# Weight sums written over the weight tiles, other step sequences and adding transfers in an encoder layer's blocked products

## The chip, the cores and the metric

The kernel runs on one core of one Trainium2 chip. The metric is the device time of one execution in microseconds (us). The engines that matter are TensorE (PE, matrix products into PSUM banks), VectorE (DVE) and ScalarE (ACT, both elementwise), GpSimd (POOL) and SyncE (SP), whose queue issues most transfers. Each engine takes its instructions in order; semaphores tie the engines together.

## The reference

One encoder layer over 256 tokens of 4096 features, all in float32. A combined projection feeds two groups of attention heads, latent attention and dilated attention; their gated outputs are mapped back and added, and a gated per-layer embedding and a last norm follow.

```python
h = rms_norm(x, g_mix[i])
proj = jnp.einsum('bsd,de->bse', h, w_in[i])
c_q, c_kv, k_rope, gate_a, q_b, k_b, v_b, gate_b = jnp.split(proj, split_idx, axis=-1)
...
y_a = rms_norm(y_a.reshape(B, S, MLA_WIDTH), g_out_mla[i]) * jax.nn.silu(gate_a)
...
y_b = rms_norm(y_b.reshape(B, S, DIL_WIDTH).astype(x.dtype), g_out_dil[i]) * jax.nn.silu(gate_b)
x = x + jnp.einsum('bse,ed->bsd', jnp.concatenate([y_a, y_b], axis=-1), w_out[i])
ple = jnp.einsum('bsc,cd->bsd', p[i], w_ple[i])
gate = jax.nn.sigmoid(jnp.einsum('bsd,de->bse', rms_norm(x, g_ple[i]), w_ple_gate[i]))
x = x + ple * gate
return rms_norm(x, g_final)
```

The widths are 4096 to 11840 columns for `w_in`, 4096 to 4096 for `w_out` and `w_ple_gate`.

## The kernel before

**Products.** Each float32 operand is split into a high part `hi` (rounded on ACT) and a low part `lo` (the rest, on DVE), and a product is three matmuls: hi by hi, hi by lo, lo by hi (`mm`, line 263). The activations are the stationary side, 128 by 128; the weights stream, 512 columns at a time.

**Blocks and steps.** A `Block` (line 1152) is 256 tokens by 1024 columns, with 32 weight rows of 128 (kt). Its four quarters are two token halves t by two column halves h. A plain step (`plain_step`, line 1194) loads one weight row (128 by 1024), converts it (one ACT instruction of 1024 columns, one on DVE) and does four products into the banks M2, X, M3 and M4. A fast pair (`fast_steps`, line 1215) takes two weight rows as a 2 by 2 matrix of 512 columns each and needs seven products instead of eight, by the Winograd form of Strassen's scheme, into M1 to M7. For that it needs four sums of weight pieces, made on DVE from the two loaded tiles into a tile T (`split1`, `split2`), and four sums of pieces of the left side, made once for a family of blocks (`add_sums`, line 1256). A pair is four steps: M1; M2 and M3; M5 and M7; M6 and M4. The first needs both loads, and both load buffers are free after the second; the last two convert from T. After the last fast step `d_mid` (line 1012), `gate_mid`, `out_mid` or `wide_mid` combine the banks M1, M5, M6 and M7 into the four quarters; after the last step `d_done` (line 1042), `gate_done`, `out_done` or `wide_done` add the other four banks.

**Order.** There are 18 such blocks: six for q, k and v of the dilated group (two of each), five gate and latent blocks, three output blocks and four of the embedding gate, with attention and smaller products between them. `spread` (line 1644) lays out the steps of a block: some plain ones as lead, then pair steps f and plain steps c mixed evenly by their cost on DVE, then plain ones as trail; e stands for the two steps of the embedding's product. The pairs per block stand in `FAST_QKV`, `FAST_G`, `FAST_O` and `FAST_P`: 3, 7, 8, 8, 8, 7; 3, 6, 7, 7, 7; 6, 7, 6; 7, 7, 7, 5. Instructions are issued by a planner that runs at build time: a clock (`Clock`, line 68) models each engine, steps are converted some steps ahead of PE (`convert_one`, line 1965), and other work is fitted in between as tasks that yield (`advance`, line 427).

**Buffers.** Weight rows are loaded by SP into four buffers `raw` of 2 by 512 columns (`fetch`, line 1951). The tile T of a pair is `T5` and `T6` in the q, k, v blocks, `B1` in the gate blocks, `B4` and `Al1` in the output blocks and `Ah2` in the last four. The high and low parts go to a ring of three tile pairs and to whatever larger tiles are free at that stage.

**Profile names.** All matmuls and most other instructions carry line 177, the helper that records them. `m`, `s`, `o` and `t` are PSUM banks, `raw` the load buffers, `hi` and `lo` the ring; `B`, `Ah`, `Al` and `T` are tiles of SBUF with their numbers left out.

Of the kernel before, what the change touches and what calls it, by code (L numbers as in the profile page):

```python
# [12 lines left out]
F32 = mybir.dt.float32  # L13
# [6 lines left out]
P = 128  # L20
S = 256
# [13 lines left out]
WARM = 6, 3  # L35

# [31 lines left out]
class Clock:  # L68


    SEEN = {"pe": 0.21, "act": 0.13, "dve": 0.125, "pool": 0.1, "sp": 0.0}

# [48 lines left out]
    def run(self, engine, us, outs, ins, late=0.0):  # L121
# [6 lines left out]
        if late:  # L128
            queue = "dma", engine
            self.free[queue] = max(self.free.get(queue, 0.0), at + 2.0) + late  # L130
            seen = self.free[queue]
        else:
            seen = at + us + self.SEEN[engine]
# [7 lines left out]
class Metered:  # L141
# [5 lines left out]
    def __getattr__(self, op):  # L147
        do = getattr(self.engine, op)

        def emit(out, *rest, **named):  # L150
# [11 lines left out]
            if op == "dma_start":  # L162
                us, late = (0.06 if key == "sp" else 1.0), out.shape[0] * size(out) * 4 / 400e3
                ins = []
# [46 lines left out]
def encoder_layer(ctx: ExitStack, tc: tile.TileContext, x, p, positions, g_mix, w_in, g_q_latent, w_uq,  # L211
# [30 lines left out]
    def plain(t):  # L242
        return t.bitcast(F32)

# [344 lines left out]
    def attend(h, q_src, k_src, pe, v, y, dil):  # L589
# [96 lines left out]
        nc.scalar.activation(y, by_token(o) if dil else o, AF.Copy)  # L686
# [16 lines left out]
    def head_unit(name, load, product, tags, done, n=2, time=48 * 0.119):  # L703
# [3 lines left out]
        def step(j):  # L707
            box = []

            def get():  # L710
                box.append(clock.made(wp.tile([P, 2, Q], F32, tag="raw", name=f"raw_{name}_{j}", bufs=RAW), "raw", RAW))
                load(box[0], j)
# [11 lines left out]
            new.ring, new.ring_id = HEADS_RING, "heads"  # L724
# [104 lines left out]
    def turn_steps(n, tags):  # L829
# [4 lines left out]
        def step(j):  # L834
            box = []

            def load():
                box.append(clock.made(wp.tile([P, 2, Q], F32, tag="raw", name=f"raw_r{n}_{j}", bufs=RAW), "raw", RAW))
# [19 lines left out]
            new.ring, new.ring_id = HEADS_RING, "heads"  # L858
# [53 lines left out]
    def gate_rest(dil, c, u):  # L912
# [6 lines left out]
        for b in range(2):  # L919
# [9 lines left out]
            for k in range(2):  # L929
                h = 4 * c + 2 * b + k  # L930
                g = G["ob" if dil else "oa"][:, h:h + 1]
                y = yb_rows(h) if dil else by_token(y_rows(ya, h))
                nc.vector.scalar_tensor_tensor(y, y, g, by_token(tp[:, k]), op0=ALU.mult, op1=ALU.mult)
# [3 lines left out]
    QUARTERS = (0, 0, "M2"), (1, 1, "X"), (0, 1, "M3"), (1, 0, "M4")  # L937

    def gate_mid(tags, blk, after=()):

        def task():
# [9 lines left out]
            for d, a, b in (((1, 1), (0, 0), "M6"), ((1, 0), (1, 1), "M5"), ((0, 1), (1, 1), "M7"),  # L951
                            ((1, 1), (0, 1), "M5")):
                nc.vector.tensor_tensor(e[d[0]][:, d[1]], e[a[0]][:, a[1]], ps[b], op=ALU.add)
# [58 lines left out]
    def d_mid(key, blk):  # L1012
        def task():
# [11 lines left out]
            yield from awaited("rx")  # L1025
            sc = [(rxq if key[0] == "q" else rx)[:, t:t + 1] for t in range(NT)]

            def add(h, t, m, old):
# [1049 lines left out]
```

## Time and profile before

| what | value |
|---|---|
| time of the runs, median (lowest to highest) | 1900.07 us (1898.4 to 1900.59), 3 runs |
| profiled execution: first to last instruction, its span | 1897.4 us |
| mean granted TensorE clock | 0.998 |
| busy: PE, DVE, ACT, POOL | 1878.5, 1696.8, 1140.2, 31.2 us |
| bytes moved by DMA | 370.59 MB |

The span runs from the first to the last instruction of the program; the profiled execution has no other time than this one. The time of a run has a little more around it, so the median stands 2.7 us above the span. Busy times are unions of an engine's instruction spans. Matmuls are pipelined and their ends are modelled, so their spans overlap and are longer than their distance.

### The profile page before, as it was taken

What the parts mean: (1) busy time and instruction counts of PE and PEld (TensorE: products, weight loads), DVE (VectorE), ACT (ScalarE), POOL (GpSimd) and SP (SyncE); (2) the same over time, 40 slices, a digit from 0 to 9 for tenths busy, and PEclk for the clock granted to TensorE, in tenths of its full rate; (3) what the DMA queues carried; (4) which work ended last, traced back from release to release, by engine and by line L of the source; (5) the groups of instructions that cost most, each with busy time, mean ns of one, the idle gap of its engine ahead of it and who ended that gap; (6) DMA issues with size and microseconds to landing.
All of it is one profiled execution on the core that took longest, in us unless ns stands there. A gap on an engine that the chain in (4) does not pass through costs nothing.

```text
span 1897.4 us, 25417 instructions
## 1 busy us (share of the span) xinstructions
PE 1878.5 (99%) x9133; PEld 1579.8 (83%) x9133; DVE 1696.8 (89%) x2354; ACT 1140.2 (60%) x1543; POOL 31.2 (2%) x41
## 2 busy tenths in 40 slices
PE   9999999999999999999999999999999999999997
PEld 7888888888899888888888999888888888888885
DVE  6999999899898989999998777999989989989897
ACT  7655656565588555556556556656655555666654
POOL 0000000000011000000000010100000000000000
PEclk9999999999999999999999999999999999999999
DMA  8666666666735566666667553576666666665665
GB/s 279 189 205 213 214 212 200 198 213 193 218 84 159 166 211 183 196 215 189 208 199 209 137 142 123 167 231 204 216 199 217 187 194 218 194 223 183 221 222 180
DMA packets 160871, 370.59 MB, mean 195 GB/s; under 512 B 29116, under 2 KB 70952, under 8 KB 160744
## 3 DMA queue, kind: packets, MB, share of 16 engines
q1 hardware_dynamic: 159896, 366.58, 62.0%
q0 software_dynamic: 512, 1.84, 0.3%
q8 instruction: 72, 1.18, 0.3%
q10 hardware_dynamic: 336, 0.54, 0.1%
q14 instruction: 55, 0.45, 0.1%
HBM read 364.72 MB, written 4.19 MB: 194 GB/s over the span
## 4 chain that ended last, share of the span: by engine, by line
PE 85%; DVE 10%; DMA 2%; issue 2%; ACT 1%; POOL 0%; DVEq 0%; ACTq 0%; POOLq 0%
PE m L177 49%; PE t L177 16%; PE s L177 11%; PE o L177 9%; DVE lo L177 3%; DVE B L177 3%; DVE T L177 2%; DVE Ah L177 1%; DMA raw<-in_w_ple_gate_dram 1%; DVE Al L177 1%; DMA raw<-in_w_in_dram 1%; ACT hi L177 0%; DVE st L177 0%; ACT B L177 0%; DVE B7b L177 0%
## 5 line engine op out<-in xcount | busy, mean ns | idle before, releaser
L177 ACT ACTIVATE hi<-raw 128x1024 fp32r<-128x1024 f32 (+2 forms) x396 | 378.9, 966 | 278.1 <-PE m L177 70.9
L177 DVE TENSOR_TENSOR lo<-raw,hi 128x1024 fp32r<-128x1024 f32 (+2 forms) x396 | 433.4, 1107 | 61.8 <-ACT hi L177 60.6
L177 PE MATMUL m<-hi,Ah 128*128 128x512 f32 (+2 forms) x659 | 247.2, 387 | 0.3 <-ACT hi L177 0.3
L177 DVE TENSOR_TENSOR B<-raw,B 128x1024 fp32r<-128x1024 f32 (+3 forms) x228 | 213.9, 947 | 20.5 <-ACT B L177 18.8
L177 PE MATMUL m<-hi,Al 128*128 128x512 f32 (+2 forms) x625 | 229.6, 380 | 0.0
L177 PE MATMUL m<-lo,Ah 128*128 128x512 f32 (+2 forms) x549 | 207.8, 379 | 1.4 <-DVE lo L177 1.3
L177 ACT ACTIVATE B<-raw 128x1024 fp32r<-128x1024 f32 (+2 forms) x142 | 135.3, 962 | 96.8 <-DMA raw<-in_w_in_dram 25.3
L177 PE MATMUL m<-hi,B 128*128 128x512 f32 (+1 forms) x524 | 179.0, 389 | 0.0
L177 PE MATMUL m<-B,Ah 128*128 128x512 f32 (+2 forms) x554 | 146.7, 359 | 0.6 <-DVE B7b L177 0.6
L177 PEld LDWEIGHTS m<-hi,Ah 128*128 128x128 f32 x659 | 124.0, 188 | 22.7 <-ACT hi L177 1.2
L177 PEld LDWEIGHTS m<-hi,Al 128*128 128x128 f32 x625 | 117.5, 188 | 21.8
L177 PEld LDWEIGHTS m<-lo,Ah 128*128 128x128 f32 x549 | 103.4, 188 | 19.9 <-DVE lo L177 2.9
L177 PEld LDWEIGHTS m<-hi,B 128*128 128x128 f32 x524 | 98.2, 188 | 19.6
L177 PEld LDWEIGHTS m<-B,Ah 128*128 128x128 f32 x554 | 95.9, 189 | 15.3 <-DVE B7b L177 1.0
L177 PE MATMUL m<-lo,B 128*128 128x512 f32 (+1 forms) x262 | 102.1, 390 | 0.1
L177 PE MATMUL m<-B,Al 128*128 128x512 f32 (+2 forms) x289 | 99.1, 371 | 0.0
L177 DVE TENSOR_TENSOR T<-raw,T 128x512 f32<-128x512 f32 (+2 forms) x110 | 85.5, 789 | 3.3 <-ACT T L177 1.7
L177 ACT ACTIVATE hi<-B 128x1024 fp32r<-128x1024 f32 x57 | 59.4, 1056 | 23.1 <-PE m L177 7.3
L177 DVE TENSOR_TENSOR lo<-B,hi 128x1024 fp32r<-128x1024 f32 x57 | 68.5, 1220 | 3.9 <-ACT hi L177 3.6
L177 PE MATMUL t<-hi,Ah 128*128 128x512 f32 x184 | 69.9, 391 | 0.0
L177 ACT ACTIVATE B<-T 128x1024 fp32r<-128x1024 f32 (+2 forms) x55 | 50.2, 916 | 22.8 <-DVE T L177 13.4
L177 PEld LDWEIGHTS m<-B,Al 128*128 128x128 f32 x289 | 54.4, 188 | 9.2
(530 smaller groups left out, 4336.9 us busy)
## 6 DMA issues: line engine op xcount, KB each, us to landing
raw<-in_w_in_dram SPq DMA_DIRECT2D x359, 512.0 KB, 4.3
raw<-in_w_out_dram SPq DMA_DIRECT2D x128, 512.0 KB, 4.6
raw<-in_w_ple_gate_dram SPq DMA_DIRECT2D x128, 512.0 KB, 4.7
raw_q<-in_w_uq_dram SPq DMA_DIRECT2D x32, 256.0 KB, 3.8
T<-in_x_dram SPq DMA_DIRECT2D x13, 512.0 KB, 6.6
raw<-in_w_in_dram SPq DMA_DIRECT2D x16, 320.0 KB, 3.1
raw_r<-in_w_uq_dram SPq DMA_DIRECT2D x16, 256.0 KB, 4.3
raw_k<-in_w_ukv_dram SPq DMA_DIRECT2D x16, 256.0 KB, 3.4
```

What stands on the lines that cost most here:

```text
L177: return do(out, *rest, **named)
```

## The change

- The four weight sums of a pair are written over the two loaded tiles: first the two sums of the first tile, once its left half has been converted, then the two of the second, once it has been converted. Signs change so that most of these are additions; `mix` and the quarter sums take the other signs.
- The tile T is no longer used for sums; its stage lends it as two more load buffers (`lend`, `give_back`), so that there are six where there were four. The load buffers are now one tile with named places, and a pair holds its two until its third and fourth step are converted. If both places adjoin, the first two sums are one instruction.
- In 23 of the pairs (letter A) the first two sums are made by a transfer that POOL issues and that adds a part of the weights onto the first tile.
- `spread` gives way to step sequences written out: c is a plain step; a or A, b, g, h are the four steps of a pair; e is the embedding's product, now last in its block. Steps of two pairs may be mixed. The pairs are 2, 8, 8, 8, 8, 8; 3, 6, 8, 7, 8; 6, 7, 6; 8, 8, 8, 5.
- In the q, k, v and latent blocks the norm's scale is taken out of the bank sums and applied to the finished quarters, on DVE or ACT. The output gain is applied where attention writes its result, so the gating is one multiplication for two heads.
- The sums of the left side take four DVE instructions instead of five; sums beyond the room of before go over parts of the left side that only plain steps use.
- The planner's clock has other landing times for transfers and a longer issue on SP.

```diff
+ORDER_D = (
+    "ccccccccccccccccccacAcbcccghbghccccc",
+    "cccaccbghAccbcaghbcghcacbcaghbghcabgahbgcahbghcc",
+    "ccccabacbgcgchacbhcghcabccAghbabgcghhabgabhghccc",
+    "ccccacbghabghccabcabgchgahbcgabghcachcbgabghhccc",
+    "ccabgccccabghhacabgbhghccccabghabcgchaabbggchhcc",
+    "ccccccabagbghhcabghacbghaAccabgcchbgcbghhabcghcc",
+)
+ORDER_G = (
+    "ccccccccccccccacbgcchacbgcacbhgchccccc",
+    "ccAcccbgcAccbhcghccaccbagabhghccbgabghchcccc",
+    "cccccabccacgcbagbghchahbgaahcbcgbhgchcabgabghhcc",
+    "cccccacbaccgbhgahacbgccAhbghbcghcabcgcahbgchcc",
+    "cccacbgaahccbgcbgcahbaghchbcgcaAbbghhcgacchbghcc",
+)
+ORDER_O = (
+    "ccaacccbbggchcahcccacbccghbcghabacgbhgcchccc",
+    "ccacbcacgchbcgcAhAbbccgghcabchcgabhcgabhghcccc",
+    "ccccabccghcabgacchbcAcghbcacbggcahhbgccchccc",
+)
+ORDER_P = (
+    "cccaccAbgcbchcgabghachbcagbgchhAAbcbcghaghbghccce",
+    "ccAbcgccabcaghhbgchacbghacbcacbcghcgaAhbgbcghhcce",
+    "cAcbccgcAcbAhbghcagcchbcgaAhbbgchghcaAbbccgghhcce",
+    "ccccacAbcghbcAcbghghabgacchbghcccc",
+)
...
+    LANDS = {"sp": 2.3, "act": 2.0, "pool": 5.7}
...
+    RAW, NEAR = 4, 0.3
+    raw_all = wp.tile([P, 2 * RAW, 512], F32, tag="raw", name="raw_all", bufs=1)
+    raw_at = {i: (raw_all, 2 * i) for i in range(RAW)}
...
+    def next_to(a, b):
+        return raw_at[a][0] is raw_at[b][0] and raw_at[b][1] == raw_at[a][1] + 2
+
+    def lend(stage, tags):
+
+        if lent["stage"] != stage:
+            give_back()
+            lent["stage"] = stage
+            for tag, n in tags:
+                t = slot(tag, [2 * n, 512])
+                for i in range(n):
+                    raw_at[lent["n"]] = t, 2 * i
+                    raw_free.append(lent["n"])
+                    lent["n"] += 1
...
+    def mix(e, ps):
+
+        nc.vector.tensor_tensor(e(1, 1), e(0, 0), ps["M6"], op=ALU.add)
+        nc.vector.tensor_tensor(e(1, 0), ps["M5"], e(1, 1), op=ALU.subtract)
+        nc.vector.tensor_tensor(e(0, 1), e(1, 1), ps["M7"], op=ALU.subtract)
+        nc.vector.tensor_tensor(e(1, 1), ps["M5"], e(0, 1), op=ALU.subtract)
...
+            nc.scalar.activation(d[0][:, 0], ps["M1"], AF.Copy)
+            mix(lambda h, t: d[h][:, t], ps)
...
-                nc.vector.scalar_tensor_tensor(d[h][:, t], blk.ps[m], sc[t], d[h][:, t], op0=ALU.mult, op1=ALU.add)
+                nc.vector.tensor_tensor(d[h][:, t], blk.ps[m], d[h][:, t], op=ALU.add)
+            yield from awaited("rx")
+            for m, t, h in quarters[2:] + quarters[:2] if key == ("v", 1) else quarters:
+                if clock.free["dve"] + 0.3 < clock.free["act"]:
+                    nc.vector.tensor_scalar(d[h][:, t], d[h][:, t], sc[t], None, op0=ALU.mult)
+                else:
+                    nc.scalar.activation(d[h][:, t], d[h][:, t], AF.Copy, scale=sc[t])
...
             def split1(hi, lo):
-                if isinstance(self.tmp, tuple):
-                    T.extend(slot(b, [2, self.q]) for b in self.tmp)
-                else:
-                    both = slot(self.tmp, [4, self.q])
-                    T.extend((both[:, :2], both[:, 2:]))
-                sub(T[0][:, 0], r[0][:, 1], r[0][:, 0])
-                sub(T[0][:, 1], r[0][:, 1], r[1][:, 1])
                 split(hi[:, 0], lo[:, 0], r[0][:, 0])
+                if dma:
+                    at = self.row(2 * j) * P
+                    nc.gpsimd.dma_start(r[0], self.w[at:at + 2 * P, self.q:2 * self.q].rearrange("(k p) n -> p k n", p=P),
+                                        accum_op=ALU.add)
 
             def split2(hi, lo):
+                if dma:
+                    split(hi, lo, r[1])
+                    return
                 nc.scalar.activation(hi, r[1], AF.Copy)
-                sub(T[1][:, 0], r[1][:, 1], T[0][:, 0])
-                sub(T[1][:, 1], r[1][:, 0], T[1][:, 0])
+                if next_to(slots[0][0], slots[1][0]):
+                    t, h = raw_at[slots[0][0]]
+                    plus(r[0], t[:, h + 1:h + 2].to_broadcast([P, 2, self.q]), t[:, h:h + 4:3])
+                else:
+                    plus(r[0][:, 0], r[0][:, 1], r[0][:, 0])
+                    plus(r[0][:, 1], r[0][:, 1], r[1][:, 1])
                 nc.vector.tensor_tensor(lo, r[1], plain(hi), op=ALU.subtract)
+                sums34()
+
+            def sums34():
+                plus(r[1][:, 1], r[1][:, 1], r[0][:, 0])
+                plus(r[1][:, 0], r[1][:, 0], r[1][:, 1])
+
+            def split3(hi, lo):
+                nc.scalar.activation(hi, r[0], AF.Copy)
+                if dma:
+                    sums34()
+                nc.vector.tensor_tensor(lo, r[0], plain(hi), op=ALU.subtract)
...
-                two(ALU.add, u[:, 0], a[:, 1], a[:, 3])
-                two(ALU.subtract, u[:, 1], u[:, 0], a[:, 0])
-                two(ALU.subtract, u[:, 2], a[:, 1], a[:, 0])
-                two(ALU.subtract, u[:, 3], a[:, 2], u[:, 1])
+                two(ALU.subtract, u[:, 0:3:2], a[:, 1:2].to_broadcast([P, 2, P]), a[:, 0:4:3])
+                two(ALU.subtract, u[:, 1], u[:, 2], a[:, 0])
+                two(ALU.add, u[:, 3], a[:, 2], u[:, 1])
...
-    FAST_QKV, LEAD_QKV = (3, 7, 8, 8, 8, 7), (18, 4, 4, 4, 4, 4)
-    FAST_G, LEAD_G = (3, 6, 7, 7, 7), (15, 10, 6, 6, 4)
-    FAST_O, LEAD_O = (6, 7, 6), (4, 5, 4)
```

269 lines of the change are left out of this document (152 added, 117 removed).

## The prediction

> **What bounds the kernel now.** I read the page first (span, busy shares), then the chain of waits in order of time, then the stages, then what PE waits for. The page:
>
> ```profile
> span 1897.4 us, 25417 instructions
> PE 1878.5 (99%) x9133; PEld 1579.8 (83%) x9133; DVE 1696.8 (89%) x2354; ACT 1140.2 (60%) x1543; POOL 31.2 (2%) x41
> PEclk9999999999999999999999999999999999999999
> ```
>
> TensorE (PE) is busy all the time, at the full clock, and VectorE (DVE) is not far behind. A busy PE could still be slow, so the chain of waits is asked for its pace (start, length, what, how many):
>
> ```profile
> 1.46 2.74 PE m L177 x6
> 195.71 6.80 PE m L177 x30
> 1617.86 16.32 PE m L177 x72
> ```
>
> The first work of PE starts at 1.46 us. Thirty matmuls of 512 columns in 6.80 us and 72 in 16.32 us, 1400 us apart: 0.2267 us each, back to back. That is PE's pace where nothing holds it. A product of this kernel is three such matmuls, 0.68 us. The stages (start:end, length, then busy us of each engine with its count):
>
> ```profile
> 100.00:500.00 400.00, 399.35 (x1761) 329.85 (x1760) 379.85 (x454) 230.94 (x250) 0.69 (x1) 1.00 0.66 207
> 500.00:650.00 150.00, 149.89 (x981) 138.29 (x980) 130.06 (x277) 108.40 (x217) 12.82 (x15) 1.00 0.49 144
> 1100.00:1300.00 200.00, 198.53 (x1106) 171.16 (x1105) 166.99 (x265) 118.51 (x191) 13.66 (x14) 1.00 0.54 169
> 1600.00:1840.00 240.00, 240.00 (x1060) 198.75 (x1059) 219.66 (x260) 145.89 (x175) 0.00 (x0) 1.00 0.65 209
> 1840.00:1897.40 57.40, 43.69 (x211) 35.77 (x210) 43.92 (x75) 27.50 (x39) 0.00 (x0) 0.93 0.56 195
> ```
>
> PE idles 0.65 us of 400 in the first stage, although DVE is busy for 379.85 of them (95%); 1.47 us of 200 in the stage where the second attention passes into the output blocks; nothing from 1600 to 1840; and 13.71 us in the last stage, the drain behind the last products, which the change leaves alone. The waits that the profile names for PE are small:
>
> ```profile
> PE m L177 <- DVE lo L177: 1.3, 3, 0.8
> PE m L177 <- DVE B7b L177: 0.9, 2, 0.6
> PE m L177 <- DVE Al L177: 0.3, 1, 0.3
> ```
>
> So the time is PE's work. The span can fall only by fewer matmuls, or by these 2.5 us of waits for DVE and little else. DVE is the second limit: a pair costs it more than it saves PE, so what DVE can carry decides how many pairs are possible.
>
> **The change, part by part.** *Pairs.* Two plain steps (two weight rows kt) are 8 products; a fast pair of steps is 7. I count one pair for each letter h in the sequences. The blocks for q, k, v go from 41 to 42, the next five from 30 to 32, the output blocks stay at 19, the last four go from 26 to 29: 116 becomes 122. Six products less, 18 matmuls at 0.2267 us: **-4.08 us** of PE. Nothing hides this, since PE is the path; the transposes and the last steps keep their matmuls.
>
> *What a pair costs DVE and ACT.* The groups by shape (count, busy us, mean ns of one):
>
> ```profile
> L177 DVE TENSOR_TENSOR lo<-raw,hi 128x1024 fp32r<-128x1024 f32 x309 | 374.0, 1220 | 59.4 <-ACT hi L177 58.3
> L177 DVE TENSOR_TENSOR lo<-raw,hi 128x512 fp32r<-128x512 f32 x77 | 52.5, 684 | 1.0 <-ACT hi L177 0.9
> L177 DVE TENSOR_TENSOR B<-raw,B 128x512 f32<-128x512 f32 x86 | 59.2, 688 | 1.5
> L177 ACT ACTIVATE hi<-raw 128x1024 fp32r<-128x1024 f32 x309 | 323.8, 1058 | 240.9 <-PE m L177 64.7 <-DMA raw<-in_w_in_dram 52.7 <-PE t L177 48.1
> L177 ACT ACTIVATE hi<-raw 128x512 fp32r<-128x512 f32 x77 | 48.0, 625 | 37.2 <-PE t L177 11.5 <-PE o L177 7.9 <-issue 7.0
> ```
>
> Before, a pair is four sums of 512 columns, one low part of 512 and three of 1024 on DVE: 4 x 0.688 + 0.684 + 3 x 1.220 = 7.10 us, against 2 x 1.220 = 2.44 us for two plain steps. So six more pairs cost DVE 6 x 4.66 = +28.0 us. On ACT they cost 6 x (0.625 + 3 x 1.058 - 2 x 1.058) = +10 us, which its 40% idle time hides.
>
> *Adding transfers.* Each letter A (4 + 4 + 3 + 12 = 23) lets a DMA make the first two sums: 23 x 2 x 0.688 = **-31.6 us** of DVE. In the other 99 pairs, where the two weight tiles adjoin, the two sums become one instruction of 1024 columns with a strided input. No row has that form; it lies between 1.220 (the plain 1024 row) and 1.376 (no gain). I take 1.220, the nearest row, in half of the pairs: 50 x 0.156 = -8 us, with 0 and -15 as ends.
>
> *The quarter sums of the seven projection blocks.*
>
> ```profile
> L177 DVE SCALAR_TENSOR_TENSOR B<-m,st,B 128x512 f32<-128x512 f32 x26 | 17.8, 742 | 0.1
> L177 DVE TENSOR_TENSOR B<-B,m 128x512 f32<-128x512 f32 x20 | 12.7, 681 | 0.1
> L177 ACT ACTIVATE B<-B,st 128x512 f32<-128x512 f32 x20 | 13.5, 708 | 0.0
> L177 DVE TENSOR_SCALAR T<-T,st 128x256 f32<-128x256 f32 x32 | 10.2, 362 | 0.6
> ```
>
> Nine scaled additions become eight plain ones: 9 x 0.742 - 8 x 0.681 = 1.23 us less per block, -8.6 us. The 28 scalings that follow go to DVE or ACT, whichever the planner's clock has free: 0.36 (a row of half the size) to 0.74 us each on DVE, 0.71 on ACT. I take half on DVE at 0.55: +8 us, ends 0 and +21. They run after the banks are free and lie beside PE. The sums of the left side (four instructions for five, one more set in two families) and one multiplication for two in the gating come to a few us either way; I set them at zero.
>
> DVE in sum: 28.0 - 31.6 - 8 - 8.6 + 8 = -12 us, 1685 of some 1892, again 89%. By block, an eight-pair block without A costs at most 8 x 7.10 + 16 x 1.22 = 76.3 us of DVE in 120 x 0.68 = 81.6 us of PE. Three blocks of before (v0, q1 and k1) have just that load, inside the stage from 100 to 500 us in which PE idles 0.65 us. So eight pairs are bearable where they are new (two gate blocks, the first three of the last family).
>
> *The adding transfer as a wait.* It is issued by POOL after the first step's split has read the tile, and the third step of the pair (g) waits for it on ACT and on DVE. Behind that wait stand all later conversions and the emptying of PSUM banks, and so PE. No row shows an adding transfer; the nearest are POOL's plain ones and their issue, beside SP's weight loads:
>
> ```profile
> T<-in_x_dram POOLq DMA_DIRECT2D x2, 512.0 KB, 5.2
> T<-in_c_dist_dram POOLq DMA_DIRECT2D x1, 512.0 KB, 4.9
> raw<-in_w_in_dram SPq DMA_DIRECT2D x359, 512.0 KB, 4.3
> L177 POOL DMA_DIRECT2D T<-in_x_dram x2: 722/732/741, 1187.0 to 1201.8; - x2
> L177 POOL TENSOR_TENSOR acc<-acc,junk 128x256 f32<-128x256 f32 x30 | 27.7, 923 | 680.4 <-ACT junk L177 680.4
> q1 hardware_dynamic: 159896, 366.58, 62.0%
> ```
>
> Not under 4.9 us, since it moves as many bytes; the upper end I set at twice 5.2 = 10.4 us, an estimate for reading the tile too. Cover: PE's time for the letters from A up to its g (c 2.72, a 0.68, b, g and h 1.36). Over the 23 it is 4.8 us once (Abcg), 6.8 once, then 7.5, 8.2, 8.8, twice 9.5, seven times 10.2, nine times more. At 6 us, which I take (5.2 to land and 0.7 to issue, the nearest rows), one A is 1.2 us late, which the next converted steps hide: **0**. At 10.4 us the lateness sums to 19 us. On POOL nothing stands near these issues but the additions of the two attention stages, 0.92 us each. In bytes 23 x 0.5 MB are 3% more on SP's queue of 366.58 MB, which keeps the DMA engines busy for 62%: nothing.
>
> The Trainium skill (DMA: Bandwidth & Descriptors, section Anatomy of one DMA) fits a POOL transfer by 2.0 us plus bytes over 436 GB/s; that would be about 3.2 us here, by which no A is late, but this trace's 4.9 and 5.2 us decide. The Trainium skill (SBUF — State Buffer, section SBUF: two separate sides) says that POOL cannot write descriptors while DVE runs an instruction in a mode that takes both its ports. The two issues in the row took 0.72 to 0.74 us in a stage where DVE is 83% busy, so no run here shows that loss, but it speaks for the rival with late transfers.
>
> *Load buffers.* A pair now keeps its two weight tiles until g and h instead of until its second step, and two more buffers are lent. The sequences have up to four such tiles open (once five) out of six, so two are left for loads that land in 4.3 us. Before it was four buffers with early release. I set this at 0; it costs up to about 1 us where four are open and plain steps follow.
>
> *Order.* Some blocks start their pairs earlier. After the first ple block the first g comes 3 x 2.72 + 0.68 + 1.36 = 10.2 us into the block (ccAbc); before, six plain steps alone were 16.3 us. That g needs the previous block's gating issued:
>
> ```profile
> 1623.39 0.68 DVE L177 SCALAR_TENSOR_TENSOR B<-B,t 128x512 f32<-128x512 f32 x1
> 1628.99 0.68 DVE L177 SCALAR_TENSOR_TENSOR B<-B,t 128x512 f32<-128x512 f32 x1
> ```
>
> The block begins at 1617.9 us. The bank that g itself uses is read until 1624.1 (6.2 us in), the last one until 1629.7 (11.8 us). So g is covered by 4 us, but conversions are pushed back by up to 11.8 - 10.2 = 1.6 us.
>
> *Waits that go.* Stages with A's have DVE time to spare; of the 2.5 us that PE waits for DVE I let 1.0 go (ends 0 and 2.5).
>
> **Sum** against the profiled span: 1897.4 - 4.08 - 1.0 = 1892.3 us. The median of the runs, 1900.07, lies 2.7 us above the span; the same difference carries over: 1900.07 - 5.1 = **1895.0 us**.
>
> **The rivals.** *Handovers give it back.* New waits appear where pairs start earlier (1.6 us after the first ple block, as much at one other block start) or where two load buffers are too few: +2 us with no wait gone, 1900.07 - 4.08 + 2 = 1898 us. For it: all 18 blocks change their order and DVE has 5 to 10% of slack. Against: PE waits nowhere from 200 to 500 us at that load. Chance 0.27.
>
> *DVE's relief counts for more.* All idle time of PE inside (1897.4 - 1878.5 = 18.9 us, less 13.7 of the last stage and 1.5 at the start) goes: 1900.07 - 4.08 - 3.7 = 1892.3 us. For it: 23 pairs lose two DVE instructions just where they are put. Against: DVE's total hardly falls. Chance 0.15.
>
> *Late transfers, the slower side.* If the adding transfer takes 10.4 us, ACT and DVE stand still for 19 us in all; I let half of it reach PE, since steps are converted ahead: +9.6 - 4.08, 1905.6 us. It decides from about 8.8 us on, where half the lateness (8.0 us) equals the gain. For it: DMA must read what it adds to, beside loads at 65% of the queues. Against: only 5 of 23 have less than 9 us of cover. Chance 0.13.
>
> **How the numbers follow.** The forecast has 0.45. A measurement of this kernel tells about 0.2% (3.8 us) from no change: the forecast and DVE's relief lie beyond it, together 0.60 faster; the handovers are 0.28 with a share of the late transfers; 0.12 slower. The forecast alone spans 1893.0 to 1896.3 (2.5 us of waits gone or none). The range takes in relief and handovers and the unknown ends of both, 1889.0 to 1902.5, and leaves out most of the late transfers.
>
> **What would show it.** Right: 18 matmuls less, pace unchanged, PE's idle time as before or less, DVE near 1685 us; adding transfers landing in 5 to 8 us, with no long wait of ACT or DVE on them. Wrong: DVE or ACT waiting on POOL's transfers for over 10 us in all; PE waiting for DVE at the starts of the second gate block or the second ple block; ACT's waits on weight loads reaching PE.

## The result, and the profile after

The changed kernel takes **1917.04 us** (1915.17 to 1917.96, 4 runs) where the kernel before takes 1899.37 us (1898.40 to 1900.59, 4 runs) on the same chip: ratio 1.0090, 95% interval 1.0076 to 1.0104. It is slower by 17.7 us; the forecast was 1895.0 and the range ended at 1902.5. Times here and below are medians of a kernel's undisturbed executions, and one further execution of the experiment e11, which took 3847.09 us for a reason that is not known, is left out of them. The page of the profile after, its span, its engines and the first line of its chain of waits:

```profile
span 1916.2 us, 25531 instructions
...
PE 1884.7 (98%) x9115; PEld 1576.1 (82%) x9115; DVE 1705.5 (89%) x2294; ACT 1158.7 (60%) x1579; POOL 58.5 (3%) x64
...
PE 52%; DVE 13%; DMA 3%; issue 3%; ACT 2%; DVEq 0%; ACTq 0%
```

and the same line of the chain in the kernel before:

```profile
PE 85%; DVE 10%; DMA 2%; issue 2%; ACT 1%; POOL 0%; DVEq 0%; ACTq 0%; POOLq 0%
```

PE's 18 matmuls are gone (9133 to 9115), as meant. DVE was to fall to 1685 us and rose from 1696.8 to 1705.5. The shares of the chain after add up to 73% only, so it is not followed back to the start. Transfers have 3% of the span in it and 2% before, which does not tell what the loss is. PE is idle for 31.5 us of the span (18.9 before), and its busy time is 6.2 us longer although it does fewer matmuls. The stages, to be held beside those of before:

```profile
100.00:500.00 400.00, 397.36 (x1744) 326.27 (x1743) 373.23 (x428) 232.54 (x260) 3.60 (x3) 1.00 0.63 206
...
1100.00:1300.00 200.00, 197.87 (x1130) 171.55 (x1131) 164.86 (x251) 119.32 (x196) 14.40 (x15) 1.00 0.53 169
1600.00:1840.00 240.00, 237.85 (x1042) 194.81 (x1041) 216.77 (x248) 147.80 (x180) 10.77 (x9) 1.00 0.76 228
1850.00:1916.20 66.20, 52.38 (x248) 43.05 (x248) 52.92 (x86) 31.24 (x43) 0.00 (x0) 0.93 0.55 188
```

From 1600 to 1840 us PE was never idle and did 1060 matmuls; now it idles 2.15 us and does 1042. From 100 to 500 us it idles 2.64 us instead of 0.65. The last stage keeps its 13.8 us. The first loads of `w_out` and of `w_ple_gate` cut the span into three parts. The first part, up to the output blocks, takes 8.4 us more than before (1156.8 for 1148.4), the output blocks, which have no pair more, take 8.5 us more (375.4 for 366.9), and the rest 2.0 us (384.0 for 382.0). What PE waits for, the first rows:

```profile
PE m L207 <- DVE lo L207: 7.6, 11, 2.0
PE m L207 <- DVE B L207: 2.8, 6, 0.7
PE s L207 <- DVE T L207: 2.0, 5, 0.8
```

All rows of PE waiting for DVE add up to 18.0 us, against 4.0 before. So PE is held up by its operands. Two things can make them late: DVE itself, or what DVE and ACT wait for.

### The profile page after: what moved, and what is told of

It is laid out like the page before. It is cut to its first block, busy times and chain, and to the rows that moved or that the text cites. A ratio compares the mean times of both kernels' runs of the same rounds, so it can differ in the third digit from the quotient of the medians.

```text
span 1916.2 us, 25531 instructions
## 1 busy us (share of the span) xinstructions
PE 1884.7 (98%) x9115; PEld 1576.1 (82%) x9115; DVE 1705.5 (89%) x2294; ACT 1158.7 (60%) x1579; POOL 58.5 (3%) x64
## 4 chain that ended last, share of the span: by engine, by line
PE 52%; DVE 13%; DMA 3%; issue 3%; ACT 2%; DVEq 0%; ACTq 0%
PE m L207 31%; PE t L207 9%; PE s L207 7%; PE o L207 5%; DVE lo L207 5%; DVE B L207 2%; DVE raw_all L207 2%; DVE T L207 1%; ACT hi L207 1%; DMA raw_all<-in_w_out_dram 1%; DMA raw_all<-in_w_ple_gate_dram 1%; DVE Al L207 1%; DVE B7b L207 1%; DVE Ah L207 1%; DMA Al<-in_w_out_dram 1%
## 5 line engine op out<-in xcount | busy, mean ns | idle before, releaser
L207 ACT ACTIVATE hi<-raw_all 128x1024 fp32r<-128x1024 f32 (+2 forms) x419 | 412.9, 998 | 226.7 <-PE t L207 45.1
L207 DVE TENSOR_TENSOR lo<-raw_all,hi 128x1024 fp32r<-128x1024 f32 (+2 forms) x419 | 476.0, 1150 | 68.7 <-ACT hi L207 66.5
L207 ACT ACTIVATE B<-raw_all 128x1024 fp32r<-128x1024 f32 (+2 forms) x146 | 143.1, 984 | 97.4 <-DVE raw_all L207 30.2
L207 DVE TENSOR_TENSOR B<-raw_all,B 128x1024 fp32r<-128x1024 f32 (+2 forms) x146 | 164.7, 1131 | 14.6 <-ACT B L207 13.7
L207 PE MATMUL m<-hi,B 128*128 128x512 f32 (+1 forms) x482 | 166.2, 391 | 0.0
L207 DVE TENSOR_TENSOR raw_all<-raw_all 128x512 f32<-128x512 f32 (+1 forms) x219 | 155.8, 712 | 6.4 <-DMA raw_all<-in_w_ple_gate_dram 0.7
L207 ACT ACTIVATE hi<-B 128x1024 fp32r<-128x1024 f32 (+1 forms) x61 | 59.9, 986 | 37.7 <-DVE B L207 12.1
L207 PE MATMUL t<-hi,Ah 128*128 128x512 f32 x206 | 77.7, 391 | 0.0
L207 DVE TENSOR_TENSOR lo<-B,hi 128x1024 fp32r<-128x1024 f32 (+1 forms) x61 | 68.5, 1132 | 4.3 <-ACT hi L207 3.8
L207 ACT ACTIVATE B<-T 128x1024 fp32r<-128x1024 f32 (+2 forms) x52 | 44.5, 856 | 40.4 <-DMA T<-in_w_in_dram 17.7
L207 PE MATMUL t<-lo,Ah 128*128 128x512 f32 x159 | 61.9, 389 | 0.0
```

The costliest lines, as they stand in the source:

```text
L207: return do(out, *rest, **named)
```

## The experiments

All kernels were timed beside the kernel before, whose medians there are 1898.86 to 1899.51 us. In the edits `A`, `a`, `b`, `g`, `h` are the letters of the step sequences, "in place" means sums over the loaded weights, "own tile" sums in T as before. P is the last stage, the four blocks of the embedding gate. The letters of the theories are those of the expectations.

| run | what it is | time, us | ratio to before, 95% interval | DVE busy, us |
|---|---|---|---|---|
| e1 | changed kernel, no adding transfers | 1938.26 | 1.0206 (1.0191 to 1.0221) | 1735.9 |
| e2 | changed kernel, the 23 transfers' sums not made | 1905.24 | 1.0031 (1.0019 to 1.0044) | 1704.3 |
| e3 | the 23 transfers copy instead of adding | 1906.76 | 1.0039 (1.0024 to 1.0054) | 1704.4 |
| e4 | old order, 116 pairs, in place, six buffers | 1909.88 | 1.0057 (1.0042 to 1.0072) | 1707.6 |
| e5 | e4 with own tile, four buffers | 1900.60 | 1.0008 (0.9999 to 1.0017) | 1690.1 |
| e6 | e5 with 122 pairs, evenly laid out | 1919.98 | 1.0111 (1.0094 to 1.0128) | 1718.5 |
| e7 | e2, ACT's conversions in g and h freed of sums | 1913.27 | 1.0077 (1.0062 to 1.0092) | 1705.8 |
| e8 | e4, the same freeing | 1908.37 | 1.0051 (1.0036 to 1.0066) | 1704.2 |
| e9 | changed kernel, DVE's sums pulled apart | 1969.09 | 1.0360 (1.0344 to 1.0375) | 1690.9 |
| e10 | e1, sums pulled apart | 1970.29 | 1.0374 (1.0357 to 1.0391) | 1716.5 |
| e11 | e4, sums pulled apart | 2011.09 | 1.0586 (1.0569 to 1.0604) | 1688.1 |
| e12 | e5, 24 pairs make their first sums twice | 1908.85 | 1.0048 (1.0033 to 1.0063) | 1717.0 |
| e13 | e5, eight pairs in three P blocks | 1910.23 | 1.0060 (1.0045 to 1.0075) | 1704.5 |
| e14 | e5, 22 pairs of P make their first sums twice | 1920.68 | 1.0115 (1.0100 to 1.0130) | 1716.4 |
| e15 | changed kernel, g two letters later after A | 1934.17 | 1.0186 (1.0169 to 1.0203) | 1708.2 |
| e16 | e6, no first sums in P | 1905.43 | 1.0033 (1.0022 to 1.0044) | 1685.7 |
| e17 | e5, first sums made in step b | 1940.86 | 1.0219 (1.0205 to 1.0233) | 1691.9 |
| e18 | e4, both loads and first sums in step a | 1909.74 | 1.0052 (1.0039 to 1.0066) | 1713.3 |

### The adding transfers: e1, e2, e3

e1 gives all first sums back to DVE, e2 leaves the transfer out, e3 lets it write without adding:

```diff
 e1: +ORDER_D, ... = ([o.replace("A", "a") for o in t] for t in (ORDER_D, ...))
 e2: -  nc.gpsimd.dma_start(r[0], ..., accum_op=ALU.add)
 e3: -  accum_op=ALU.add)
     +  )
```

> All 23 adding transfers are gone; their sums are made on DVE, 31.6 us more of its work; sequences, lent buffers and sums in place stay. Theory L (late adding transfers are most of the 23 us of new stalls): 1900 to 1908 us, held back only by DVE. Theory O (the sequences and the buffers held longer are the cause): 1912 us or more, since nothing of that has changed.

> The 23 pairs keep their short form on DVE, but the adding transfer itself is left out (their first two sums are missing from the result). Theory L: the stalls behind the transfers go and DVE keeps its relief, 1893 to 1903 us. Theory O: 1910 us or more.

> The 23 transfers stay, with their issue and the waits for them, but copy instead of adding (so 23 pairs have wrong first sums). Theory L with the adding as what makes them slow: they land in 5 to 6 us and the time falls to 1900 to 1908 us. If it is POOL's way of issuing or the loads beside them, they still land in 8 us and more, and the time stays at 1913 to 1918 us. Theory O: 1912 us or more with either landing.

The page's line of the engines, of e1 and then of e2:

```profile
PE 1891.9 (98%) x9115; PEld 1578.5 (82%) x9115; DVE 1735.9 (90%) x2339; ACT 1160.8 (60%) x1579; POOL 30.7 (2%) x41
```

```profile
PE 1878.2 (99%) x9115; PEld 1575.5 (83%) x9115; DVE 1704.3 (90%) x2294; ACT 1162.9 (61%) x1579; POOL 30.8 (2%) x41
```

With the same order and the same matmuls, 31.6 us of DVE (e1 less e2) are worth 33.0 us of time, so in this order DVE's load is paid nearly in full. Two other things differ in e1: the 23 pairs make their second sums one step earlier, and the mean granted clock of TensorE is 0.994 (0.998 in e2). The clock stood at 0.50 for four stretches of 3.4 us inside e1's span, each beginning within 1 us of the end of a wait of PE of 1.9 to 2.9 us; that is 6.8 us of the 33.0 at most. Against e1 the adding transfers win 21.2 us; against sums that cost nothing (e2) they lose 11.8 us, and copying transfers (e3) lose only 1.5, which the intervals do not tell from nothing. It is the adding that is late. Transfers issued by POOL in the changed kernel (count, size, median us to landing):

```profile
raw_all<-in_w_ple_gate_dram POOLq DMA_DIRECT2D x8, 512.0 KB, 8.2
raw_all<-in_w_in_dram POOLq DMA_DIRECT2D x5, 512.0 KB, 7.9
Ah<-in_w_ple_gate_dram POOLq DMA_DIRECT2D x4, 512.0 KB, 8.0
T<-in_w_in_dram POOLq DMA_DIRECT2D x3, 512.0 KB, 9.8
raw_all<-in_w_out_dram POOLq DMA_DIRECT2D x3, 512.0 KB, 9.4
```

and the same ones in e3, as copies:

```profile
raw_all<-in_w_ple_gate_dram POOLq DMA_DIRECT2D x8, 512.0 KB, 5.5
raw_all<-in_w_in_dram POOLq DMA_DIRECT2D x5, 512.0 KB, 4.8
...
raw_all<-in_w_out_dram POOLq DMA_DIRECT2D x3, 512.0 KB, 7.0
```

One by one, the 23 adding transfers land 6.0 to 12.4 us after the start of their issue, median 8.6; as copies 3.7 to 7.8, median 5.6. The changed kernel's timeline (start, length, in brackets the idle time before) shows one of them, in `Accbcag`:

```profile
118.32 1.20 POOL L207 DMA_DIRECT2D T<-in_w_in_dram  x1 [53.82 <-DVE lo L207]
...
127.31 0.69 DVE L207 TENSOR_TENSOR raw_all<-raw_all,T 128x512 f32<-128x512 f32 x1 [3.61 <-DMA T<-in_w_in_dram]
127.32 1.06 ACT L207 ACTIVATE B<-T 128x1024 fp32r<-128x1024 f32 x1 [4.34 <-DMA T<-in_w_in_dram]
```

The transfer took 8.9 us and g reached ACT 4.3 us and DVE 3.6 us before it was done. From its issue ACT had come through the five letters between A and g in 4.7 us and DVE in 5.4, not in the 10 that PE needs for them. Over the 23 transfers, ACT stands 21.2 us and DVE 6.6 us in waits that the profile puts down to them; in e3 it is 2.7 us and none.

### Longer cover: e15

```diff
+def later(order, by=2.5):
...
+    for j in range(len(kind)):
+        g[j][0] = max(g[j][0] + by * (kind[j] == "A"), g[j - 1][0] + 0.01 if j else 0)
+        h[j][0] = max(h[j][0], g[j][0] + 1.0, h[j - 1][0] + 0.01 if j else 0)
```

The g of each pair with A goes two places back in the sequence, and its h stays behind it.

> The changed kernel with step g of the 23 pairs that have an adding transfer moved two letters later (h after it, the order among pairs kept, so some move by one letter only); nothing else. Two letters are some 2.5 to 4 us on the converting engines, and the transfers land 8.6 us after their issue where the waits for them are 2 to 5 us. Theory L (the 12 us that after has over the kernel without the transfers are waits of ACT and VectorE for landings): 4 to 8 us of them go, 1909 to 1914. Rival H (the buffers held two letters longer make loads late by as much, or the shift only moves the crowding): 1915 to 1923.

A miss: 17 us slower than the changed kernel. The waits on the adding transfers did shrink, on ACT from 21.2 to 8.1 us and on DVE from 6.6 to 1.8. But ACT's waits for all transfers grew from 163 to 186 us, so those for ordinary weight loads grew by 36. One such row, first of the changed kernel, then of e15:

```profile
ACT B L207 <- DMA raw_all<-in_w_in_dram: 16.6, 16, 2.5
```

```profile
ACT B L228 <- DMA raw_all<-in_w_in_dram: 33.1, 24, 3.3
```

The pair's two buffers come free later, and later steps crowd (`gghh`). With these sequences and six buffers, two letters of distance cost more than the lateness. Which of the two, held buffers or crowding, weighs more was not separated.

### The order, and the sums in place: e4, e5, e6, e7, e8

e4 puts the old `spread` and the 116 pairs into the changed kernel, without A. e5 then takes the sums back to a tile of their own, with four load buffers; e6 is e5 with the change's 122 pairs:

```diff
 e4: +ORDER_D = [spread(*x) for x in zip((3, 7, 8, 8, 8, 7), ...)]
 e5: -plus(r[0][:, 0], r[0][:, 1], r[0][:, 0])
     +plus(T[0][:, 0], r[0][:, 1], r[0][:, 0])
     ...
 e6: +ORDER_D = [spread(*x) for x in zip((2, 8, 8, 8, 8, 8), ...)]
```

> The changed kernel with the step order of before, 116 pairs and no adding transfer: sums in place, lent buffers and the new quarter sums alone. Theory L and theory O: 1895 to 1902 us, about as before or a little less by DVE's relief. Theory B (holding the weight tiles longer costs loads even in the old order): 1905 us or more.

> As the run with the old order and 116 pairs, but the weight sums go to a tile of their own again, the first two already in the pair's first step, with four load buffers. Theory C (sums over the raw tiles make a chain: ACT must wait for sums that must wait for ACT): back to 1896 to 1900 us. Theory K (the planner's clock, the new quarter sums and the scaling passes cost the 11 us): 1906 us or more.

> As the run before, but with the 122 pairs of the change, spread evenly by the old rule, no adding transfer. If DVE can carry six more pairs out of place: 1892 to 1898 us. If DVE is the limit (28 us more work on it): 1903 us or more.

e7 and e8 let ACT's conversions in g and h read another finished tile of the same size, so that ACT need not wait for the sums:

```diff
-nc.scalar.activation(hi, r[0], AF.Copy)
+nc.scalar.activation(hi, other(), AF.Copy)
```

> The changed kernel without transfers, and ACT's conversion in the third and fourth step of a pair reads another tile of the same size that is long ready (so the result is wrong), while DVE's work and the holding of the load buffers stay as they are. Theory C: 1893 to 1898 us, 7 to 12 us under the 1905 us of the run without transfers. If the sequences or the longer holding of buffers cost those 10 us: 1902 us or more.

> The same edit in the run with the old order and 116 pairs (1909.9 us). Theory C: 1896 to 1901 us. Otherwise 1906 us or more.

e5 is as fast as the kernel before: the quarter sums, the scalings, the gating, the sums of the left side and the planner's clock together change nothing that can be told, and take 6.7 us off DVE. e4 is 9.3 us slower than e5 at the same pairs and order, with 17.5 us more on DVE: the sums in place cost. e6 is 19.4 us slower than e5, with 28.4 us more on DVE and 18 matmuls less: the six pairs cost too. e7 and e8 speak against a chain from DVE's sums to ACT: ACT's waits for DVE fall from 364 us in e4 to 161 in e8 and from 271 in e2 to 163 in e7, and yet e8 is only 1.5 us faster than e4 and e7 is 8.0 us slower than e2. Why e7 loses is open. Nor are loads what e4 lacks: ACT waits 44 us for transfers there and 161 in e5.

Where e4's DVE time comes from shows in its timeline:

```profile
249.40 1.42 DVE L234 TENSOR_TENSOR raw_all<-raw_all 128x512 f32<-128x512 f32 x2
250.74 1.22 DVE L234 TENSOR_TENSOR lo<-raw_all,hi 128x1024 fp32r<-128x1024 f32 x1
251.99 1.42 DVE L234 TENSOR_TENSOR raw_all<-raw_all 128x512 f32<-128x512 f32 x2
```

and in e5's:

```profile
267.30 1.29 DVE L234 TENSOR_TENSOR T<-raw_all 128x512 f32<-128x512 f32 x2
...
269.18 1.23 DVE L234 TENSOR_TENSOR lo<-raw_all,hi 128x1024 fp32r<-128x1024 f32 x1
270.32 2.55 DVE L234 TENSOR_TENSOR T<-raw_all,T 128x512 f32<-128x512 f32 x3
```

Instructions on DVE overlap a little: a sum is 0.69 us long, and the next one can start 0.60 us after it started. The low part that begins at 250.74 is followed at 251.99, 1.25 us later, by a sum that overwrites what it reads; in e5 the next one starts 1.14 us after it. Two first sums in place take 1.42 us together, where the second overwrites what the first reads, and 1.29 us in a tile of their own. Counted from start to start, 249 of e4's sums of 512 columns that read no bank are followed after 0.71 to 0.73 us and nearly all others after 0.60 or 0.61; in e5 it is 143. Every one of these 249 and 143 is followed by an instruction that waits for the semaphore that the sum raises; among those followed after 0.60 or 0.61 us only 2 and 3 are. Low parts of 1024 columns followed after 1.24 to 1.30 us are 169 in e4 and 70 in e5. That is 106 times 0.12 and 99 times 0.11, some 24 us of DVE's time. The busy time shows less of it, since it counts lengths: 0.69 for 0.60 us of a sum and 1.22 for 1.14 of a low part, some 17 us, which is the 17.5 of e4 less e5. Merged sums save little, since they are few, 10 of 116 pairs in e4 and 11 of 99 in the changed kernel, of which the largest group is:

```profile
L207 DVE TENSOR_TENSOR raw_all<-raw_all 128x1024 f32<-128x1024 f32 x9 | 11.0, 1220 | 0.1
```

### Pulling the sums apart: e9, e10, e11

If the spacing is the cost, the low parts can be put between the sums. In step b:

```diff
                     plus(r[0][:, 0], r[0][:, 1], r[0][:, 0])
+                    nc.vector.tensor_tensor(lo, r[1], plain(hi), op=ALU.subtract)
                     plus(r[0][:, 1], r[0][:, 1], r[1][:, 1])
```

and in step g:

```diff
                 nc.scalar.activation(hi, r[0], AF.Copy)
-                if dma:
-                    sums34()
+                plus(r[1][:, 1], r[1][:, 1], r[0][:, 0])
                 nc.vector.tensor_tensor(lo, r[0], plain(hi), op=ALU.subtract)
+                plus(r[1][:, 0], r[1][:, 0], r[1][:, 1])
```

> The changed kernel with the four VectorE sums of a pair pulled apart so that no VectorE instruction follows directly on one whose operand it overwrites or whose result it reads: the lo subtraction of the second tile stands between the two first sums, and the two second sums move to step g, around its lo subtraction. Nothing else changes, the same instructions are issued. In the trace the sums that overwrite follow their forerunner at 0.72 us where 0.61 us is their spacing elsewhere, and the lo after them at 1.25 us instead of 1.14. Theory D (the end is set by VectorE's busy time plus some 200 us of idle time that cannot be used): up to 0.35 us in each of the 99 pairs goes, VectorE falls by 15 to 34 us from 1705, and the time falls to the floor set by PE (about 1895) plus what the late adding transfers still cost (about 11): 1906, between 1900 and 1911. Rival S (the place of the sums in the order, buffers held until step g, is what costs, not VectorE's time): the second sums come even later, 1917 to 1922.

> The same pulling apart with all first sums on VectorE, no adding transfers (e1 was 1938 us with VectorE at 1736). Theory D: VectorE falls by 20 to 40 us and the time follows it one to one: 1898 to 1918, about 1908. Rival S: 1935 to 1942. If it comes out under the changed kernel, then the adding transfers bought nothing that the order of the VectorE sums would not have.

> The same pulling apart in the kernel with the old order and 116 pairs, sums over the raw weights, no adding transfers (e4 was 1909.9 with VectorE at 1707.6). Theory D: VectorE falls to 1670 to 1690 and the time to PE's floor for 116 pairs, 1898 to 1901. Rival S: 1908 to 1914.

All three missed: theory D's figures by 60 to 110 us, and rival S, which had the sign, named a few us at most. DVE's busy time fell as expected, by 14.6, 19.4 and 19.5 us, so the spacing is what makes sums in place dear on DVE. But the time rose, so these runs do not show what the spacing alone costs in time. From e11's timelines, DVE's and then ACT's:

```profile
262.98 0.68 DVE L234 TENSOR_TENSOR raw_all<-raw_all 128x512 f32<-128x512 f32 x1
264.87 1.83 DVE L234 TENSOR_TENSOR lo<-raw_all,hi 128x1024 fp32r<-128x1024 f32 x2 [1.21 <-ACT hi L234]
```

```profile
263.78 1.58 ACT L234 ACTIVATE hi<-raw_all 128x1024 fp32r<-128x1024 f32 x2 [1.97 <-DVE raw_all L234]
```

The last sum now stands at the end of g; ACT's conversion for h waits for it, and DVE's low part for h, next on DVE, waits for ACT. Each pair can pay a round trip in which both engines stand. ACT's waits for DVE are 364 us in e4 and 575 in e11. Here the chain that e7 and e8 speak against for the order of the change is real. So theory D's rule of thumb, that the span lies some 200 us above DVE's busy time, held from e1 to e8 (199 to 208 us) and fell here (251 to 322).

### What a microsecond of DVE costs, and where: e12, e13, e14, e16

The same pairs, order and PE work as e5, with first sums made twice, spread over the kernel (e12) or in the last stage P alone (e14):

```diff
 plus(T[0][:, 0], r[0][:, 1], r[0][:, 0])
 plus(T[0][:, 1], r[0][:, 1], r[1][:, 1])
+for _ in range(2 * (j == 2 or j == 5 and self.name in ("y_sums", "x1_sums"))):
+    plus(T[0][:, _], r[0][:, 1], r[_][:, _])
```

The condition of e14 is that the block belongs to P and the pair isn't its first. e13 lays eight pairs instead of seven into P's first three blocks, and e16 leaves out P's first sums in e6.

> The kernel with sums in a tile of their own, the old order and 116 pairs (e5, 1900.6 us, VectorE 1690), with the two first sums made twice in 24 pairs: the result is the same, PE does the same work, VectorE has about 29 us more. Theory D: the time becomes 1719 + 200 = 1919, between 1912 and 1924, though not one matmul was added; this is what the six more pairs did (e6, 1920). Rival O (the six pairs cost by crowding the order, not by VectorE's time): 1899 to 1904, since 200 us of idle VectorE time absorb them.

> The kernel with sums in a tile of their own, the old order and 116 pairs (e5, 1900.6 us), with eight pairs instead of seven in the first three blocks of the last stage P (ple_gate) only: three pairs more, PE 2.0 us less, VectorE about 14 us more, all of it in P. Theory F (what counts is VectorE's work block by block, and P is full at seven): the cost is P's part of what e6 lost, 262 to 272 us from load to load, so about 10 us: 1911, between 1907 and 1914. Rule T (the whole span counts, at e12's rate of 0.3 us for each us of VectorE): 1903, between 1900 and 1906.

> As e12 (first sums made twice, result and PE work the same), but with all of the ballast in P: 22 pairs there, about 27 us of VectorE, the same amount as e12 spread over all stages at a cost of 8 us. Theory F: nearly all of it becomes time, 1900.6 + 22 = 1922, between 1916 and 1928. Rule T: as e12, 1906 to 1912.

> The kernel with sums in a tile of their own and 122 pairs (e6, 1920 us, VectorE 1718) with the first two sums of the pairs in P left out (29 pairs, the step g converts another, finished tile of the same size; the output is wrong for that), VectorE 35 us less. Theory F: P falls back to PE's pace and the rest of e6's loss stays: 1920 - 12 = 1908, between 1904 and 1912. Rule T (whole span: 1683 + 200 is under PE's floor): 1895 to 1900, faster than the kernel before by the 4 us of PE work.

e12 came out between the theories: 26.9 us of DVE cost 8.3. With that open, theory F (block by block) was set against a rule over the whole span, and all three runs lie in F's ranges and outside T's: 1910.23 for 1911, 1920.68 for 1922, 1905.43 for 1908. 26.3 us of DVE in P cost 20.1 us, without one matmul more. The stretches of P in e5 and in e14 (columns as in the stages):

```profile
1520.00:1610.00 90.00, 89.98 (x402) 73.82 (x402) 80.61 (x106) 51.23 (x62) 0.00 (x0) 1.00 0.62 204
1610.00:1700.00 90.00, 90.00 (x399) 74.53 (x398) 82.00 (x95) 55.28 (x65) 0.00 (x0) 1.00 0.63 207
1700.00:1785.00 85.00, 85.00 (x377) 70.38 (x376) 77.83 (x91) 52.46 (x62) 0.00 (x0) 1.00 0.63 204
```

```profile
1520.00:1620.00 100.00, 95.24 (x416) 76.02 (x415) 89.86 (x121) 54.20 (x64) 0.00 (x0) 1.00 0.57 190
1620.00:1710.00 90.00, 87.18 (x379) 70.33 (x378) 85.45 (x103) 51.03 (x61) 0.00 (x0) 1.00 0.59 193
1710.00:1805.00 95.00, 92.16 (x401) 74.51 (x400) 87.95 (x106) 55.01 (x65) 0.00 (x0) 1.00 0.59 194
```

In e5 PE is not idle at all, and DVE is busy for 240.4 of 265 us, 91%. That looks like 25 us of room, and it is not: with 26 us more PE makes 1196 matmuls in 285 us instead of 1178 in 265. DVE is then at 92%. The idle time that is left hardly gives way: DVE stands 18.3 us waiting for ACT in e5's stretches and still 17.1 in e14's. ACT's waits grow instead, for DVE from 20.0 to 42.0 us and for loads from 34.0 to 53.2. That this mutual waiting is what keeps DVE's room from use is argued from these rows, not tested.

### Place or form of the sums: e17, e18

e4 and e5 differ in the tile, in the step that makes the first sums and in the number of load buffers. e17 and e18 cross the first two:

- e17 is e5 with the two first sums, still into T, moved from `split1` to `split2`. The first load buffer comes free after b.
- e18 is e4 with both loads of a pair fetched for step a and the two first sums moved from `split2` to `split1`.

> The kernel with sums in a tile of their own, the old order and 116 pairs (e5, 1900.6 us, VectorE 1690), with the first two sums moved from step a to step b, where the kernel with sums over the weights makes them (e4, 1909.9 us, VectorE 1707.6), and in e4's order of VectorE instructions; the first load buffer comes free one step later for that. Theory W (the writing over itself costs: VectorE starts the next instruction 0.11 us later where it overwrites an operand of the one before): VectorE stays near 1690 and the time near e5's, 1899 to 1903. Theory Q (the later place of the first sums costs, since step g's conversion comes soon after): 1906 to 1912.

> The kernel with sums over the weights, the old order and 116 pairs (e4), with both loads of a pair fetched for step a and the first two sums made there, after the split of the left half, as e5 makes them. Theory W: VectorE stays at some 1700 to 1708 and the time near e4's, 1905 to 1911. Theory Q: as e5, 1899 to 1903.

e18 stands with e4: in place costs the same 9 us in either step, though DVE's busy time is 5.7 us higher (1713.3). e17 fits neither theory. Its DVE time (1691.9) is e5's, as W said, but it takes 40 us longer. ACT's waits for DVE are 328 us there (157 in e5) and for transfers 196 (161). Two things are dear together: the first of four buffers is held for a step more, and the sums are made just ahead of their conversion. How the 40 us split between the two is open, and so is whether it is the six buffers that spare e4 this.

None of the eighteen beats the kernel before; e5 equals it.

## Why the prediction was wrong, by its own steps

Two steps failed, the load that DVE can carry and the price of the adding transfers. The parts of the span, cut as above at the first loads of `w_out` and `w_ple_gate` (us, from the profiled executions):

| run | up to `w_out` | output blocks | P and the end |
|---|---|---|---|
| before | 1148.4 | 366.9 | 382.0 |
| changed | 1156.8 | 375.4 | 384.0 |
| e2, transfers' sums not made | 1151.5 | 370.6 | 381.7 |
| e4, old order, 116 pairs, in place | 1152.3 | 374.7 | 382.5 |
| e5, the same, own tile | 1149.0 | 367.2 | 381.6 |
| e6, own tile, 122 pairs | 1155.8 | 369.6 | 392.2 |
| e13, own tile, eight pairs in P | 1149.3 | 368.2 | 391.0 |

**"The time is PE's work", with DVE as a second limit that its share shows.** For the kernel before this stands. The first step that failed is the next one, "eight pairs are bearable where they are new". It carried DVE's load in three blocks of the q, k, v stage (95% busy, PE never late) over to blocks of P and the gates. e13 tests it for P: three blocks from seven to eight pairs cost 9.6 us, though PE has 9 matmuls less. For the blocks ahead of the output e6 shows it: three more pairs there cost 6.8 us over e5. A stage that runs at 95% does not show what another one can carry at 91%. In the changed kernel the loss does not stand in P, whose 12 transfers take 16.5 us of sums (12 x 2 x 0.688) off DVE: P is 2.0 us longer than before, and the rest stands ahead of it, 8.5 us of it in the output blocks without a pair more.

**-4.08 us of PE.** The matmuls went; the time they stood for was refilled. "Nothing hides this" was wrong: a matmul saved is worth its time only while DVE keeps up.

**A pair's cost on DVE, +28.0 us.** e6 less e5: 28.4. Right. **23 adding transfers, -31.6 us.** e1 less e2: 31.6. Right. **Quarter sums, scalings and gating, -0.6 in all.** e5 less before: -6.7, inside the ends given.

**Merged first sums, -8 us.** Mis-sized: the tiles adjoin in 11 of 99 pairs, not half, which by the same 0.156 us is -1.7. Beside it a term is missing. The next instruction on DVE starts 0.11 to 0.12 us later where it waits for the one before, and sums in place make it wait more often. Both together are +17.5 us of DVE and 9.3 us of time (e4 less e5); in the table most of that, 7.5 us, falls in the output blocks. The mean lengths of single instructions (0.690 us in place, 0.688 before) do not show it, only the distance between starts does. So DVE is at 1705.5, not 1685: -31.6 + 28.4 - 6.7 + 17.5 on 1696.8 gives 1704.4.

**The adding transfer at 6 us, cost 0.** This is the second step that failed. The cost is 11.8 us (changed kernel less e2). Landing was mis-sized (8.6 us in the median, inside the ends of 4.9 and 10.4, but up to 12.4), and the cover was counted on the wrong engine. PE's time from A to g is not what stands between the issue and the wait: ACT and DVE convert ahead of PE and passed the letters between in half the time in the one case shown. The prediction's own sign of being wrong, over 10 us of waits on these transfers, came up with 21.2 us on ACT and 6.6 on DVE. The rival with late transfers had the mechanism and +9.6 us at 10.4 us of landing. That its size comes near 11.8 is in part luck, since the lateness was counted against PE's cover; the condition it was given (from 8.8 us on) fell with that, and so its chance of 0.13. Its time, 1905.6 us, was missed too, since it knew nothing of DVE's load. The 3.2 us estimated from the Trainium skill's fit (DMA: Bandwidth & Descriptors, section Anatomy of one DMA) do not hold here: even copies issued by POOL took 5.6 us, and the measurement decides. Nor do the issues show the loss that the Trainium skill (SBUF — State Buffer, section SBUF: two separate sides) names for POOL's descriptors beside a DVE instruction that takes both ports: most of e3's copies are issued in 0.72 us, as POOL's plain transfers were before.

**Load buffers, 0.** In the changed kernel this is not refuted: ACT's waits for ordinary loads are 142 us, against 182 before. e15 shows that no room is left: with g two letters later they are 178 us and the time is 17 us longer, though held buffers and crowding were not told apart. **Order, 1.6 us pushed back, waits that go, -1.0.** PE's waits for DVE rose from 4.0 to 18.0 us instead. What the written-out sequences cost by themselves no run shows: e1 is 18.3 us slower than e6, with the sequences and the sums in place changed together.

In sum: the changed kernel with the first sums of its 23 pairs for free (e2) is 10 us above the forecast, and the late transfers add 11.8 us. Together that is the miss of 22 us. For the 10 us there are two causes that the runs show one by one, six more pairs (19.4 us, e6 less e5) and sums in place (9.3 us, e4 less e5), both with more work on DVE; how much of each is in the 10 us, and how much the new sequences add or save, is open. The forecast had neither part.

## What to carry to other kernels

Headroom on a second engine is a property of a stage: measure it by adding dead work there (e14), rather than by reading the busy share elsewhere. A transfer's cover is counted on the engine that will wait for it, which here runs ahead of the one that ends the kernel. Compare a change stage by stage as well: here the output blocks lost 8.5 us although they got no pair more. Before sums are moved into their operands' place, look at the starts of neighbouring instructions and not at their mean lengths.

## What was not expected of the hardware

- An adding transfer of 512 KB issued by POOL lands 8.6 us after its issue starts (median of 23), a copying one 5.6. The issue itself is longer too. POOL's rows in the changed kernel and in e3 (count, busy us, mean ns):

```profile
L207 POOL DMA_DIRECT2D raw_all<-in_w_ple_gate_dram x8 | 9.6, 1262 | 186.6 <-DVE Al L207 158.6 <-DVE B L207 15.8 <-DVE lo L207 12.2
```

```profile
L207 POOL DMA_DIRECT2D raw_all<-in_w_ple_gate_dram x8 | 5.8, 722 | 188.5 <-DVE Al L207 159.2 <-DVE B L207 16.7 <-DVE lo L207 12.7
```

- A DVE instruction that waits for the one just before it, because it overwrites its operand or reads its result, starts 0.11 to 0.12 us later than one that does not (0.72 against 0.60 us after a sum of 512 columns in e4 and e5, 1.25 against 1.14 after a low part of 1024).
- Behind some waits of PE of about 2 us the granted clock fell. It stood at 0.50 for 3.4 us right after a wait of 2.0 us in the changed kernel (at 1466.7 us), and at four waits of 1.9 to 2.9 us in e1. In e15 two waits of 1.9 and 2.6 us had no such stretch behind them.
